# Joint seven-product pairs over both sequences for the mixing projections of an encoder layer

## The chip, the cores and the metric

One core of a Trainium2 chip runs the whole layer. The metric is device microseconds of one execution, and the median of three executions is given. A profile comes from one more execution, traced by the hardware profiler.

## What is computed

The layer works on two sequences of 512 tokens with 1024 channels, each by itself but with the same weights, in float32. Cut to what matters here:

```python
x = x + 0.5 * swiglu(rms_norm(x, ffn1_norm), ...)          # D_FF = 2816
h = rms_norm(x, mix_norm)
aq, ak, av, mq, mk, mv, gate_pre, o_pre, g_att, g_mlstm = split(h @ w_in)
#   widths 512 128 128 512 512 512 16 512 1024 1024
att = gqa_block_attention(rope(rms(aq)), rope(rms(ak)), av)  # 8 heads of 64, 2 key heads
mem = mlstm_bidirectional(mq, mk, mv, gate_pre, gate_bias, o_pre, head_norm)   # 4 heads of 128
merged = sigmoid(g_att) * (att @ w_up_att) + sigmoid(g_mlstm) * (mem @ w_up_mlstm)
x = x + merged @ w_out
x = x + 0.5 * swiglu(rms_norm(x, ffn2_norm), ...)
```

mlstm_bidirectional ends with a norm per head, a per-channel weight (head_norm) and sigmoid(o_pre) as a gate.

## The kernel before

**Matrix products.** A float32 operand is split in two parts, hi and lo, and a product is the sum of three TensorE matmuls (hi·hi, hi·lo, lo·hi) of 128x128 by 128x512. Activations lie transposed, channels on partitions, so a column block of 128 output channels over one sequence is 8 x 3 = 24 matmuls. The split is one ACT copy and one DVE subtraction. Split weights that are wanted again are parked in DRAM by load_w (L247) and fetched back by the second sequence.

**The order.** First loads and transposes, then the first FFN up (class Up, `product` at L333), FFN down (L589), then mix(0) and mix(1), which are generators for the two sequences, interleaved by hand at the end of the kernel, then the second FFN. Both FFNs take the two sequences together and use the seven products of Strassen and Winograd in place of eight half-size products: the sequences are one axis of the 2x2 split, the halves of the 1024 input channels the second, and two column blocks the third. Their operands are the split tiles `xc[B11]`, `xc[B21]`, `xc[B22]`, `xc[T1]` to `xc[T4]`, split from normalised rows by `put` (L278 on ACT, L279 on DVE). Each product is 12 matmuls. An Up object keeps the results of some blocks that it began early in DRAM.

**mix.** The first sequence's rows come out of FFN down one column block at a time. There they are only scaled by the norm's channel weight and split into `xh`, `xl` (emit_hl, L143); the factor per token (`r[s]`, and `R[s]` for the transposed layout) is applied where a projection leaves PSUM. The squares for the norm are taken by ACT (L152) and added by POOL (L156). Then follow, per sequence:

- kv and gates (272 columns) and q (512 columns) by tok_proj, tokens on partitions (L739);
- rope on q and k (L787 to L808, L928), transposes to `qT` and `kst`;
- attention, eight heads: scores (L989 to L1004: matmuls at L995, the maximum over a row of 512 at L998, exponentials at L1000, the reciprocal at L1001 and the scaling at L1002), then attend (L1006 to L1032: transposes at L1014, split of what they give at L657 by ACT and L658 by DVE, matmuls at L1021);
- mLSTM, four heads: mask rows out of DRAM (L961), mem_head (L1098; exponentials at L1122, products with the scores at L1124), mem_out (L1141, matmuls at L1157, square at L1159, normalisation to L1164);
- merges (merge_att, merge_mem), the projection `w_up` of attention and memory, gated;
- the output projection in eight units (out_unit, L1188).

The 28 column blocks of `w_in` (8 of the attention gate, 8 of the memory gate, 4 of the output gate, 8 of the mLSTM's q and k) go through proj and proj_w (L755). They are units, of which each has a load and a computation. `go` runs units with the load one unit ahead, and `queue` with `fill(n)` puts n units between other work. This is how the blocks lie between the heads of attention and mLSTM:

```python
queue.extend(att_gate(d) for d in range(KD))
queue.extend(out_gate(h) for h in range(2))
Ps = scores(0)
for h in range(HA):
    nxt = scores(h + 1) if h + 1 < HA else None
    attend(h, Ps)
    Ps = nxt
    mem_max(h // 2, h % 2)
    fill(1 if h < 4 else 2)
```

Engines take their instructions in the order of a scheduler's priorities; `shifted(n)` moves what is under it by n places. All DMAs are issued by SP.

## Time and profile before

| | |
|---|---|
| median of three executions | 2101.9 us (2101.75 to 2104.15) |
| profiled execution | 2103.76 us, span 2101.90 us |
| mean granted TensorE clock | 0.996 |
| PE busy | 2067.3 us, 98% of the span, 9488 matmuls and transposes |
| DVE, ACT, POOL busy | 1577.5, 895.6, 104.6 us |

Of a group the profile gives the line, engine, operation, output and input tiles, shapes and count, then busy time and the mean of one, and behind the second bar the idle time of the engine in front of the group and what ended it. A line of the timeline has the start and the length in us, then the same names; a bracket holds the idle time before it and its releaser. A row of windows has the stretch, its length, the busy time (and number of instructions) of PE, PEld, DVE, ACT and POOL, then the granted clock, the share of DMA and GB/s.

By the timeline, FFN down ends at 658 us and the second FFN's products begin at 1448.75. Between these lie, as far as they can be parted: kv and q of the first sequence 658 to 693, its rope and attention to 828, its mLSTM and merges to 1011, kv and q of the second to 1044, the output projection of the first and rope of the second to 1113, attention of the second to 1222, its mLSTM to 1346, memory gate and merge to 1405, and its output projection.

### The profile page before, as it was taken

To read this page: it belongs to the slowest core of one execution; us is meant where nothing else is said; L and a number is where in the kernel's file an instruction comes from. 1 tells how busy PE (TensorE), PEld (TensorE's weight loads), DVE (VectorE), ACT (ScalarE), POOL (GpSimd) and SP (SyncE) were. 2 spreads that over 40 slices of the span, in tenths; PEclk is the share of its full clock that TensorE was granted. 3 is DMA by queue.
4 is the path that set the end of the run, shared out by engine and by line. 5 is a ranking of instruction groups with operands and counts; after the bars stand their busy time and mean duration, and the time that the engine had idled before them with its cause. 6 is when DMAs were issued, how large, how long until landed. Compare 5 with 4: busy or idle time off the path is not lost.

```text
span 2101.9 us, 27326 instructions
## 1 busy us (share of the span) xinstructions
PE 2067.3 (98%) x9488; PEld 1693.5 (81%) x9488; DVE 1577.5 (75%) x2864; ACT 895.6 (43%) x1643; POOL 104.6 (5%) x112
## 2 busy tenths in 40 slices
PE   8999999999999999999999999999999999999997
PEld 6888888888888777878887787788888888888886
DVE  7888888786797898575568745554888888786796
ACT  6544444442234566463344543323544444442222
POOL 0000000001003011000110000001000000000000
PEclk9999999999999999999999999999999999999999
DMA  8655655699767654778585354677656555599752
GB/s 275 203 172 191 194 176 177 210 353 343 262 228 253 203 186 161 252 255 277 186 291 178 103 171 144 216 243 239 206 170 224 179 183 181 179 353 341 268 191 110
DMA packets 304186, 458.53 MB, mean 218 GB/s; under 512 B 20304, under 2 KB 170848, under 8 KB 303024
## 3 DMA queue, kind: packets, MB, share of 16 engines
q1 hardware_dynamic: 303456, 455.52, 64.4%
q0 software_dynamic: 592, 1.27, 0.3%
q8 instruction: 75, 1.23, 0.2%
q14 instruction: 63, 0.52, 0.1%
HBM read 289.82 MB, written 166.89 MB: 217 GB/s over the span
## 4 chain that ended last, share of the span: by engine, by line
PE 91%; DVE 5%; DMA 2%; ACT 1%; issue 1%; SPq 0%; POOL 0%; DVEq 0%; ACTq 0%; POOLq 0%
PE pss L333 17%; PE mm L755 17%; PE pst L333 11%; PE mm L333 11%; PE mm L589 8%; PE pst L589 4%; PE pss L589 4%; PE mm L739 4%; PE pso L589 3%; PE pso L1021 1%; PE pso L739 1%; PE pst L1014 1%; PE pso L1157 1%; PE pss L995 1%; PE pst L755 1%; PE pss L755 1%
## 5 line engine op out<-in xcount | busy, mean ns | idle before, releaser
L755 PE MATMUL mm<-xh,w 128*128 128x512 f32 x896 | 291.5, 395 | 0.5 <-DMA w<-wpark 0.5
L333 PE MATMUL pss<-xc,w 128*128 128x512 f32 x1056 | 256.2, 391 | 0.7 <-DVE t L364 0.7
L333 PE MATMUL mm<-xc,w 128*128 128x512 f32 x1056 | 253.0, 390 | 2.5 <-DVE xc L279 1.0
L333 PE MATMUL pst<-xc,w 128*128 128x512 f32 x1056 | 253.6, 389 | 0.0
L333 PEld LDWEIGHTS pss<-xc,w 128*128 128x128 f32 x1056 | 196.9, 188 | 47.9 <-DVE t L364 7.3
L333 PEld LDWEIGHTS mm<-xc,w 128*128 128x128 f32 x1056 | 197.4, 188 | 45.4 <-DVE w L292 1.5
L333 PEld LDWEIGHTS pst<-xc,w 128*128 128x128 f32 x1056 | 198.2, 188 | 41.2
L755 PEld LDWEIGHTS mm<-xh,w 128*128 128x128 f32 x896 | 167.8, 189 | 34.0 <-DMA w<-wpark 1.2
L589 PE MATMUL mm<-rt,w 128*128 128x512 f32 (+1 forms) x819 | 187.7, 383 | 0.0
L755 PE MATMUL mm<-xl,w 128*128 128x512 f32 x448 | 176.3, 394 | 0.0
L589 PEld LDWEIGHTS mm<-rt,w 128*128 128x128 f32 x819 | 150.6, 188 | 29.8
L291 ACT ACTIVATE w<-t 128x512 fp32r<-128x512 f32 x176 | 107.0, 627 | 139.1 <-issue 55.2
L292 DVE TENSOR_TENSOR w<-t,w 128x512 fp32r<-128x512 f32 x176 | 118.2, 687 | 54.9 <-ACT w L291 53.0
L333 PE MATMUL pss<-xc,f 128*128 128x512 f32 x528 | 126.8, 389 | 0.0
L333 PEld LDWEIGHTS pss<-xc,f 128*128 128x128 f32 x528 | 99.1, 188 | 20.6
L657 ACT ACTIVATE w<-wr 128x512 fp32r<-128x512 f32 x72 | 45.2, 632 | 137.7 <-PE pso L589 71.8
L755 PEld LDWEIGHTS mm<-xl,w 128*128 128x128 f32 x448 | 84.4, 188 | 16.2
L657 ACT ACTIVATE w<-t 128x512 fp32r<-128x512 f32 x82 | 51.8, 632 | 107.3 <-PE pst L589 62.4
L589 PE MATMUL pst<-rt,w 128*128 128x512 f32 x396 | 93.7, 389 | 0.0
L589 PE MATMUL pss<-rt,w 128*128 128x512 f32 x396 | 93.7, 389 | 0.0
L239 ACT ACTIVATE w<-wr 128x1024 fp32r<-128x1024 f32 (+1 forms) x56 | 57.2, 1028 | 71.8 <-PE mm L755 34.0
L589 PEld LDWEIGHTS pss<-rt,w 128*128 128x128 f32 x396 | 74.3, 188 | 15.4
(331 smaller groups left out, 3686.9 us busy)
## 6 DMA issues: line engine op xcount, KB each, us to landing
rt<-rbuf SPq DMA_DIRECT2D x154, 512.0 KB, 5.3
wpark<-w SPq DMA_DIRECT2D x104, 512.0 KB, 3.2
w<-wpark SPq DMA_DIRECT2D x104, 512.0 KB, 4.9
wr<-in_ffn_w_gate_dram SPq DMA_DIRECT2D x62, 512.0 KB, 5.5
rbuf<-tab SPq DMA_DIRECT2D x102, 256.0 KB, 4.1
wr<-in_ffn_w_up_dram SPq DMA_DIRECT2D x44, 512.0 KB, 4.6
rbuf<-f SPq DMA_DIRECT2D x72, 256.0 KB, 4.0
wr<-in_w_in_dram SPq DMA_DIRECT2D x36, 512.0 KB, 6.5
```

What stands on the lines that cost most here:

```text
L239: pin(nc.scalar.activation(hi, raw, AF.Copy))
L291: pin(nc.scalar.activation(t[:, 0], src, AF.Copy))
L292: pin(V_.tensor_tensor(t[:, 1], src, f(t[:, 0]), op=ALU.subtract))
L333: nc.tensor.matmul(p, a[:, k, :], xt[:, b, k, :], start=(first and k == 0 and i == 0), stop=(k == HK_ - 1 and i == 2), skip_group_check=True)
L589: nc.tensor.matmul(p, u[:, a, d * P:(d + 1) * P], r[:, b, ts], start=(first and q == 0 and k == 0), stop=(q == len(us) - 1 and k == 2), sk ...
L657: nc.scalar.activation(hi, src, AF.Copy)
L739: nc.tensor.matmul(p[b][:, :N], a[:, k, bs], w_[:, kl, :], start=(k == 0 and i == 0), stop=(k == KD - 1 and i == 2))
L755: nc.tensor.matmul(p, a[:, k, :], b, start=(k == 0 and i == 0), stop=(k == n - 1 and i == 2))
L995: nc.tensor.matmul(p, qT[:, h, b * P:(b + 1) * P], kv[:, hk * 2 + j, :], start=(j == 0), stop=(j == 1))
L1014: nc.tensor.transpose(p[:, b * P:(b + 1) * P], Ps[b][:, kb * P:(kb + 1) * P], ident)
L1021: nc.tensor.matmul(po, Vst[:, kv_, hk, :], w, start=(kv_ == 0 and i == 0), stop=(kv_ == 3 and i == 1))
L1157: nc.tensor.matmul(po, vm[:, a, t, hs_], b, start=(t == 0 and n == 0), stop=(t == 3 and n == 2))
```

## The change

The 28 column blocks leave mix. A new class Joint, derived from Up, computes them in a stage of its own between the first FFN and mix, as 14 pairs of blocks over both sequences, seven products to a pair; nine pairs are begun early on `xc[B11]` and `xc[B21]` alone. Gate blocks leave it as tanh of half their value, q and k blocks split in hi and lo, all into DRAM (`agbuf`, `mgbuf`, `ogbuf`, `qkbuf`). Attention and mLSTM fetch them from there.

For this the rows are normalised in place before the stage, so the factor per token goes from all later evictions. done1 takes the first sequence's norm at the end of FFN down and writes `xc[B11]`, `xc[B21]`; the second sequence's statistics follow behind the first pair's first products. The lower half of the second sequence's rows, which the stage uses only in sums, is saved split in DRAM (`xlbuf`) and fetched afterwards. kv and q of both sequences are then computed together, q and k of the second resting unrotated in `rawbuf`; mLSTM's values of the second sequence come next (they fill rope of the first, and rest in `vbuf`), and those of the first are the filler of its attention, in two halves (tok_halves). Output units of the first sequence are the filler in rope (four) and attention (three) of the second. The `1 +` of the output gate and head_norm move from POOL into two DVE instructions of mem_out. An added one-element exponential in `gates` is to have ACT's table loaded before attention. The rest of the second FFN is the same.

```diff
+    QK_, TANH_ = 0, 1
+    JOINT = 9
+    class Joint(Up):
...
+            n = len(blocks)
+            begun, whole = list(range(JOINT - LAST)), list(range(JOINT, n))
+            self.order = [j for p in zip(begun, whole) for j in p]
+            self.order += begun[len(whole):] + whole[len(begun):] + list(range(JOINT - LAST, JOINT))
...
+        def out(self, j, i, s, src, row=None):
+            _, kind, to = self.blocks[j][i]
+            lo = src if row is None else row
+            if kind == TANH_:
+                nc.scalar.activation(lo, src, AF.Tanh, scale=0.5)
+                nc.sync.dma_start(to(s), lo)
+                return
+            hi = self.ring("o")
+            nc.scalar.activation(hi.bitcast(F32R), src, AF.Copy)
+            V_.tensor_tensor(lo.bitcast(F32R), src, hi, op=ALU.subtract)
+            nc.sync.dma_start(to(s)[:, 0, :], hi)
+            nc.sync.dma_start(to(s)[:, 1, :], lo)
...
+        def begin(self, j, W):
+            self.kept[j] = kept[j][0]
+            t = self.ring("o")
+            X = gu_first_a(W, self.xc, t)
+            nc.sync.dma_start(kept[j][0], t)
+            self.begun()
+            self.open = j, X, W
+        def begun(self):
+            if self.open:
+                j, X, W = self.open
+                product(X, W[B21], self.xc[B21], False)
+                self.out(j, 0, 0, X, self.ring("o"))
+            self.open = None
...
+            Y, Z = PS(), PT()
+            second = lambda: product(Y, W[T2_], xc[T2_], True)
+            v1 = got or ring("v")
+            if got:
+                second()
+            else:
+                X = gu_first_a(W, xc, v1)
+                second()
+                product(X, W[B21], xc[B21], False)
+                with shifted(SOONER):
+                    self.out(j, 0, 0, X, ring("h"))
+            u2, v5 = ring("h"), ring("v")
+            with shifted(SOONER):
+                V_.tensor_tensor(u2, v1, Y, op=ALU.add)
+            product(Z, W[T1], xc[T1], True)
+            with shifted(SOONER):
+                nc.scalar.activation(v5, Z, AF.Copy)
+            mid()
+            product(Y, W[T3], xc[T3], False)
+            with shifted(SOONER):
+                V_.tensor_tensor(v5, v5, Y, op=ALU.add)
+            with shifted(SOONER):
+                V_.tensor_tensor(v5, v5, v1, op=ALU.add)
+            self.out(j, 1, 1, v5)
+            product(Z, W[B22], xc[B22], False)
+            with shifted(SOONER):
+                V_.tensor_tensor(u2, u2, Z, op=ALU.add)
+            self.out(j, 0, 1, u2)
+            product(Y, W[T4], xc[T4], False)
+            with shifted(SOONER):
+                V_.tensor_tensor(v1, v1, Y, op=ALU.add)
+            self.out(j, 1, 0, v1)
...
+    KK = 2
+    KORDER = (4, 6, 0, 2)
+    def tok_load(cols, k0):
+        return load_w([win_v[:, k0:k0 + KK, c:c + n] for c, n in cols], ("in", cols[0], k0))
+    def tok_part(p, x, w, k0, blocks, N):
+        for kl in range(KK):
+            xh, xl = x(k0 + kl)
+            for b in blocks:
+                bs = slice(b * P, (b + 1) * P)
+                for i, (a, w_) in enumerate(((xh, w[0]), (xh, w[1]), (xl, w[0]))):
+                    nc.tensor.matmul(p[b][:, :N], a[:, bs], w_[:, kl, :],
+                                     start=(k0 == KORDER[0] and kl == 0 and i == 0),
+                                     stop=(k0 == KORDER[-1] and kl == KK - 1 and i == 2))
...
+            for x, p in zip(xs_, ps_):
+                tok_part(p, x, w, k0, range(4), N)
+            if k0 == KORDER[-1]:
+                for done, p in zip(dones, ps_):
+                    for b in range(4):
+                        done(b, p[b])
...
+    def tok_halves(x, cols, done):
...
+        def comp(half, k0):
+            blocks = (2 * half, 2 * half + 1)
+            if k0 == KORDER[0]:
+                p.update((b, MM()) for b in blocks)
+            tok_part(p, x, ws[k0], k0, blocks, N)
+            if k0 == KORDER[-1]:
+                for b in blocks:
+                    done(b, p[b])
+        return [((lambda h=h, k0=k0: load(h, k0)), (lambda _, h=h, k0=k0: comp(h, k0)))
+                for h in range(2) for k0 in KORDER]
...
-    OUT = 3
-
-    def mix(s, xh, xl, early=None, extra=None, after=None):
-
-        xsrc = lambda k: (xh[:, k, :], xl[:, k, :])
+    def mix(s, rope_fill, att_fill, extra=None, after=None):
...
+        def v_done(b, p):
+            hi, lo = [F2(F32R) for _ in range(2)] if s else (vm[:, 0, b, :], vm[:, 1, b, :])
+            split(p, hi, lo)
+            if s:
+                for i, t in enumerate((hi, lo)):
+                    nc.sync.dma_start(vbuf[:, i, b, :], f(t))
+        qks, ogs = {}, {}
+        def mem_fetch(h):
+            qks[h] = wpool.tile([P, 4, S], F32R, tag="w8", bufs=4, name=nm("qk"))
+            nc.sync.dma_start(f(qks[h]), qkbuf[s][h])
+            ogs[h] = T2(F32, "ac")
+            nc.sync.dma_start(ogs[h], ogbuf[s][:, h, :])
...
-        go(*tok_proj(xh, xl, [(512, 256), (2304, 16)], 2, kv_done))
-        if early:
-            early()
-        go(*tok_proj(xh, xl, [(0, 512)], 2, q_done), mem_qk(0, 0))
-        yield None
+        yield kv_done, k_rope, q_done, v_done
+        if s:
+            k_rope()
         gates()
-        k_turn()
+        if not s:
+            k_turn()
         for b in range(4):
+            if s:
+                qraw.append(raw_row(b))
             q_rope(b)
-        yield None
-        go(mem_qk(0, 1), mem_qk(1, 0), mem_qk(1, 1))
...
+        queue.extend(att_fill)
+        fill(1)
         Ps = scores(0)
         for h in range(HA):
             nxt = scores(h + 1) if h + 1 < HA else None
             attend(h, Ps)
             Ps = nxt
             mem_max(h // 2, h % 2)
-            fill(1 if h < 4 else 2)
-            if h == 2 and extra:
+            fill(1)
+            if h == 3 and extra:
                 extra()
         mem_scales()
         fill(99)
+        for d in range(KD):
+            nc.sync.dma_start(mg[:, d, :], agbuf[s][:, d, :])
+        for h in range(2):
+            mem_fetch(h)
...
+        def gate_fetch(d):
+            t = ths[d] = T2()
+            nc.sync.dma_start(t, mgbuf[s][:, d, :])
...
-            V_.tensor_tensor(og, og, po, op=ALU.mult)
+            V_.scalar_tensor_tensor(og, og, 1.0, po, op0=ALU.add, op1=ALU.mult)
             rh = rstd_cols(col_sums(h2), 4, DM)
-            Rh = bcast_psum(rh)
-            V_.tensor_tensor(og, og, Rh, op=ALU.mult)
-            split(og, mem[:, h, 0, :], mem[:, h, 1, :])
+            with shifted(160):
+                Rh = bcast_psum(rh)
+                V_.scalar_tensor_tensor(og, og, hn[:, h:h + 1], Rh, op0=ALU.mult, op1=ALU.mult)
+                split(og, mem[:, h, 0, :], mem[:, h, 1, :])
...
         for h in range(HM):
             Ts = mem_head(h)
-            if h == 0:
-                go(*mem_values())
             queue.append(merge_att(2 * h))
             fill(1)
             mem_out(h, Ts)
             if h + 2 < HM:
-                queue.extend([out_gate(h + 2), mem_qk(h + 2, 0), mem_qk(h + 2, 1)])
+                mem_fetch(h + 2)
             queue.append(merge_att(2 * h + 1))
             fill(99)
 
         mh, ml = A([P, KD, S], F32R, "mh"), A([P, KD, S], F32R, "ml")
-        go(*[mem_gate(d) for d in range(KD)])
         go(*[merge_mem(d) for d in range(KD)])
-        flush()
-        yield None
...
     def done1(s, d, _):
-        if s == 0:
-            if d == 0:
-                nhl[0] = xhl_tiles()
-            emit_hl(xs[0][:, d, :], gm, d, *nhl[0])
         nc.sync.dma_start(xbuf[s][:, d, :], xs[s][:, d, :])
         accs[s] = sq_add(xs[s][:, d, :], accs[s], "R")
         if s == 0 and d == KD - 1:
-            mid_stats(0, 100, 140)
-
-    def mid_stats(s, a=0, b=0):
-        with shifted(a):
-            r[s] = stats(accs[s])
-        with shifted(b):
-            R[s] = bcast_cols(r[s])
-
-    r = [None, None]
-    R = [None, None]
-
-    def prep1(d):
-        if d == 0:
-            nhl[1] = xhl_tiles()
-        xt = T2(F32, "f2")
-        nc.sync.dma_start(xt, xbuf[1][:, d, :])
-        emit_hl(xt, gm, d, *nhl[1])
+            with shifted(100):
+                r = stats(accs[0])
+            with shifted(140):
+                R = bcast_cols(r)
+                xc[B11], xc[B21] = xc_tile(), xc_tile()
+                for k in range(KD):
+                    normed(xs[0][:, k, :], gm, R, k)
+                    put(xc[B11 if k < HK_ else B21], k % HK_, xs[0][:, k, :])
...
-    m0 = mix(0, *nhl[0], None, lambda: mid_stats(1), prep1)
-    for _ in range(3):
-        next(m0)
...
+    def qk_block(h, i):
+        return (768, 1280)[i] + h * P, QK_, lambda s: qkbuf[s][h][:, 2 * i:2 * i + 2, :]
+    def tanh_block(c, buf, d):
+        return c + d * P, TANH_, lambda s: buf[s][:, d, :]
+    blocks = [[tanh_block(2832, agbuf, d + i) for i in range(2)] for d in range(0, KD, 2)]
+    blocks += [[tanh_block(3856, mgbuf, d + i) for i in range(2)] for d in range(0, KD, 2)]
+    blocks += [[tanh_block(2320, ogbuf, d + i) for i in range(2)] for d in range(0, HM, 2)]
+    blocks += [[qk_block(h, i) for i in range(2)] for h in range(HM)]
+    up = Joint(xc, blocks)
+    W = [up.left(0)]
+    up.begin(0, W[0])
+    r1 = stats(accs[1])
+    W += [up.left(j) for j in (1, 2)]
+    R1 = bcast_cols(r1)
+    up.begin(1, W[1])
+    up.begin(2, W[2])
+    for i in (B22, T1, T2_, T3, T4):
...
+    for k in range(HK_):
+        x0l, x0u, x1l, x1u = [xs[s][:, k + i * HK_, :] for s in range(2) for i in range(2)]
+        normed(x1l, gm, R1, k)
+        normed(x1u, gm, R1, k + HK_)
+        for j in ((3,), (4, 5), (6,), (7, 8))[k]:
+            up.begin(j, up.left(j))
+        put(xc[B22], k, x1u)
+        t3, t4 = up.ring("x"), up.ring("x")
+        V_.tensor_tensor(x0l, x1l, x0l, op=ALU.subtract)
+        V_.tensor_tensor(t3, x1u, x1l, op=ALU.subtract)
+        V_.tensor_tensor(x1u, x1u, x0l, op=ALU.subtract)
+        V_.tensor_tensor(t4, x0u, x1u, op=ALU.subtract)
+        put(xc[T1], k, x0l)
+        put(xc[T2_], k, x1u)
+        hi, lo = up.ring("s"), up.ring("s")
+        split(x1l, hi.bitcast(F32R), lo.bitcast(F32R))
+        nc.sync.dma_start(xlbuf[:, 0, k, :], hi)
+        nc.sync.dma_start(xlbuf[:, 1, k, :], lo)
+        later.append((T3, k, t3))
+        later.append((T4, k, t4))
...
+    up.rest(raw0)
...
-    m1 = mix(1, *nhl[1], None, lambda: stats2(0), prep2)
-    next(m1)
-    next(m0)
-    next(m1)
-    acc2[0] = next(m0)
-    next(m1)
-    next(m1)
-    acc2[1] = next(m1)
+    def extra():
+        acc2[0] = outs0[1][0]
+        stats2(0)
+    box()
+    ms = [mix(s, fills[0][s], fills[1][s], (None, extra)[s], (None, prep2)[s]) for s in range(2)]
+    (kv0, kr0, q0, v0), (kv1, kr1, q1, v1) = [next(m) for m in ms]
+    go(*tok_proj(src, [(512, 256), (2304, 16)], (kv0, kv1)))
+    go(*tok_proj(src, [(0, 512)], (q0, q1)))
+    first, *units = tok_proj(src[1:], [(1792, 512)], (v1,))
+    go(first)
+    kr0()
+    fills[0][0][:3] = [[u] for u in units]
+    fills[1][0].extend(tok_halves(src[0], [(1792, 512)], v0))
+    outs0 = next(ms[0])
+    go(*outs0[0][:1])
+    fills[0][1][:] = [[u] for u in outs0[0][1:5]]
+    fills[1][1].extend(outs0[0][5:])
+    box()
+    outs1 = next(ms[1])
+    go(*outs1[0])
+    flush()
+    acc2[1] = outs1[1][0]
```

217 lines of the change are left out of this document (118 added, 99 removed).

## The prediction

> **What bounds the kernel now.** I read the page first, then the chain of waits, then busy time by windows over the mixing part.
>
> ```profile
> L755 PE MATMUL mm<-xh,w 128*128 128x512 f32 x896 | 291.5, 395 | 0.5 <-DMA w<-wpark 0.5
> ...
> L755 PE MATMUL mm<-xl,w 128*128 128x512 f32 x448 | 176.3, 394 | 0.0
> ```
>
> These are the matmuls of the 28 column blocks, one of the page's largest groups, with next to no idle time in front. The 395 ns is the latency of one matmul, not its price. The price comes from the chain of waits, where a long unbroken stretch stands:
>
> ```profile
> 1405.39 43.52 PE mm L755 x192
> ```
>
> 43.52/192 is 226.7 ns per 128x512 matmul. So a removed matmul is worth 0.2267 us where PE alone sets the pace. The windows tell where it does:
>
> ```profile
> 658.00:693.00 35.00, 34.85 (x199) 30.44 (x197) 20.34 (x44) 18.62 (x34) 12.65 (x17) 1.00 0.97 329
> 693.00:828.00 135.00, 129.60 (x651) 102.36 (x649) 125.26 (x258) 80.12 (x159) 14.68 (x11) 1.00 0.54 175
> ...
> 1113.00:1222.00 109.00, 104.32 (x508) 83.04 (x506) 82.90 (x188) 55.07 (x119) 0.70 (x1) 0.98 0.42 136
> ```
>
> The columns are PE, PEld, DVE, ACT, POOL, clock, DMA. 658 to 693 is kv and q of the first sequence: PE alone, as in the output projection of the second, the 43.52 us above. 693 to 828 is rope and attention of the first sequence, with ten column blocks as filler between the heads: DVE is busy 125.26 of 135 us, so here DVE sets the pace and PE is full only because filler lies in the gaps. In the second attention (1113 to 1222) DVE has 82.90 of 109: PE sets it. The part that changes lies between these rows of the timeline:
>
> ```profile
> 658.03 0.41 PE L739 MATMUL mm<-w,xh 128*128 128x272 f32 x2
> ...
> 1448.75 2.88 PE L333 MATMUL mm<-xc,w 128*128 128x512 f32 x12
> 1452.45 0.66 PE L203 MATMUL pst<-ident,R 128*128 128x128 f32 x4 [0.82 <-POOL R L156]
> 1452.86 0.94 PE L333 MATMUL mm<-xc,w 128*128 128x512 f32 x3
> ```
>
> From 658.0 (first kv matmul) to 1448.7 (second FFN) are 790.7 us. Four transposes cost 0.41 (1452.45 to 1452.86). I take the rest of the program as unchanged and build the same stretch anew.
>
> **What is removed.** The 28 blocks are 28 x 2 x 24 = 1344 matmuls, the two L755 rows above (896+448). Seven products for a pair over both sequences are 7 x 12 = 84, 14 pairs 1176. That is 168 fewer, 168 x 0.2267 = 38.1 us. This is the whole gain, and it holds only if PE is as full afterwards. It cannot be: the blocks were the filler of attention and of the mLSTM heads, and they move to a stage of their own (266.6 us). I therefore go through the stages.
>
> **Seam after the first FFN.** Before, the first sequence's projection starts on unnormalised x, with the scale applied afterwards, and the second's statistics are wanted much later. Now the new stage needs normalised x at once. ACT and POOL at that place before:
>
> ```profile
> 657.55 1.34 ACT L239 ACTIVATE w<-wr 128x544 fp32r<-128x544 f32 x2 [4.51 <-PE pso L589]
> 658.79 0.62 ACT L152 ACTIVATE R<-xs 128x512 f32<-128x512 f32 x1
> ...
> 659.54 11.75 POOL L156 TENSOR_TENSOR R<-R,f 128x512 f32<-128x512 f32 x7 [12.75 <-ACT R L152]
> ```
>
> ACT stood behind a weight split that waits for the last FFN matmuls to free a weight buffer; only then came the first square of the second sequence, and POOL needed 11.75 us for seven additions (1.68 each), to 671.3. The changed program's order has the same two weight splits (now 128x1024, two of them) ahead of that square, then squares that wait for POOL to free their buffers, and between these the first copy into xc, and on PE the transposes of the second sum right behind 13 matmuls of the new stage. By these rows: first square at 660, additions end at 672; the first xc copy stands behind two squares that wait for two additions, 664. PE idles 658 to 664.4, does 13 matmuls, idles again until 672. That is 14 us with 3 us of work, 11 lost, and 1 more where the T1 weights are ready late. **12 us.** Bounds: 2 if the squares are not held up, 16 if the whole of the chain from 656 to 672 lies bare.
>
> A gap of that length has a second price:
>
> ```profile
> 1120.12 0.85 PE L995 MATMUL pss<-kv,qT 128*128 128x512 f32 x2 [4.47 <-ACT t L1000]
> ...
> 1120.60:1123.90 3.30, 3.30 (x11) 2.49 (x10) 3.30 (x9) 1.70 (x6) 0.00 (x0) 0.50 1.02 388
> ```
>
> After 4.47 us idle (the gap in brackets) the granted clock was 0.50 over the 3.3 us from 1120.60 on, a loss of about 1.7. At the seam the first such stretch would run into the wait for POOL and cost nothing, the second may or may not come; the 12 stands, with 1.7 more in the bound. [...]
>
> **New stage.** 1176 x 0.2267 = **266.6**. A pair costs 19.0 us (84), a pair begun earlier 13.6 (60). By the program's order DVE has 9 splits and sums of 512 elements, 5 additions, at most one split of 1024 and, for q/k pairs, 4 more splits. DVE prices, from one start to the next in the timeline:
>
> ```profile
> 765.71 1.27 DVE L998 TENSOR_REDUCE asm<-pss 128x1 f32<-128x512 f32 x2
> 766.91 1.27 DVE L658 TENSOR_TENSOR t<-pst,t 128x512 fp32r<-128x512 f32 x2
> ...
> 770.62 0.21 DVE L1001 RECIPROCAL asm<-asm 128x1 f32<-128x1 f32 x2
> 770.75 0.15 DVE L171 TENSOR_SCALAR rs<-rs 128x4 int32<-128x4 int32 x1
> 770.81 0.48 DVE L1002 TENSOR_SCALAR t<-t,asm 128x512 f32<-128x512 f32 x1
> 771.21 0.16 DVE L173 TENSOR_SCALAR rs<-rs 128x4 int32<-128x4 int32 x1
> ```
>
> Two maxima of 512 elements took 1.20 (765.71 to 766.91), so 0.60 each, and the two splits behind them, at 1.27 with the last one's tail, no more; the scaling took 0.40 (770.81 to 771.21), a reciprocal about 0.07. Thus at most 18 x 0.60, and 1.2 for the split of 1024, 12 us against 13.6 to 19.0: hidden. The results' DMAs, 1 to 2 MB a pair, are hidden by the same 19 us.
>
> **kv and q of both sequences.** Two of the 35 us windows: **70**.
>
> **Attention of the first sequence.** Filler now: the value projection of both sequences, 96 matmuls each; by the program's order the first fills rope, of the second half lies in heads 0 to 2, the other half behind the last scores, because the value tile waits for q's buffer. Heads 3 to 7 have none. A head's DVE work: 4 maxima, 4 splits, 1 addition, 2 gate maxima, half a split, 11.5 x 0.60, 4 x 0.40, 4 x 0.08 = 8.8 us, against PE's 16 matmuls (3.6) and 16 transposes (1.6). The scaling was slower in this stage:
>
> ```profile
> L1002 DVE TENSOR_SCALAR t<-t,asm 128x512 f32<-128x512 f32 x32 | 19.7, 619 | 0.1
> ...
> L657 ACT ACTIVATE t<-pst 128x512 fp32r<-128x512 f32 x32 | 18.9, 595 | 13.3 <-PE pst L1014 12.3 <-DVE asm L998 1.0
> L240 DVE TENSOR_TENSOR w<-wr,w 128x1024 fp32r<-128x1024 f32 x13 | 16.1, 1235 | 0.8 <-ACT w L239 0.8
> ```
>
> 619 against 480 ns adds 0.6 a head. Behind the last scaling DVE waits for transposes (0.41) and ACT's copy (0.60), with no other work queued: 0.9. Period 10.3, eight heads 82; entry 28 (21.8 of value matmuls, 12 groups of transposes, 5), exit 5: **115**. The other way: 135 before, less 13 weight splits (16.1), 17 gate and q/k passes (10.2), plus 8 value splits (4.8) and 4 weight splits (5.0) gives 118.5. Bounds 103 (8.8 a head) and 122.
>
> **mLSTM of the first sequence.** Three blocks a head, two heads, and the value projection are gone as filler; what is left is 24 merge matmuls a head. What a head takes with little filler, from 1308 on:
>
> ```profile
> 1309.58 0.29 DVE L1124 SCALAR_TENSOR_TENSOR t<-pss,t 128x128 f32<-128x128 f32 x1
> ...
> 1324.63 0.28 DVE L1124 SCALAR_TENSOR_TENSOR t<-pss,t 128x128 f32<-128x128 f32 x1
> ...
> 1345.76 0.69 DVE L1164 TENSOR_TENSOR box<-box,pst 128x512 f32<-128x512 f32 x1 [0.20 <-PE pst L213]
> ```
>
> ```profile
> 1323.82 5.96 ACT L1122 ACTIVATE t<-box,st 128x128 f32<-128x128 f32 x20
> ...
> 1340.51 0.60 ACT L1159 ACTIVATE t<-pso 128x512 f32<-128x512 f32 x1 [1.34 <-PE pso L1157]
> ```
>
> 15.05 us lie between two heads' first products on DVE, and 17.3 from the start of a head's 20 exponentials to the end of its square on ACT (1341.1), behind which a next head's exponentials would stand, as they do in the changed order. Some work of other kinds lay in between, so I take 16.2, and 7 from the last square to the end of the last split, two DVE passes behind 1345.76. 4 x 16.2 + 7 = 71.8; 69 of the 96 merge matmuls stand behind that on PE's queue, 15.7: **87.5** (82 to 93).
>
> **The rest.** Five output blocks (27.2) and 12 groups of transposes (4.9) cover rope of the second sequence: **33**, with 1 of loss. Attention of the second: 9.4 of DVE a head (the mask addition is on DVE here), 0.9 of wait, 82, exit 4: **86** (75 to 109). mLSTM as above plus the mask rows:
>
> ```profile
> L961 DVE TENSOR_TENSOR box<-box,tab 128x512 f32<-128x512 f32 x6 | 4.1, 689 | 10.0 <-DMA box<-ebuf 10.0
> ```
>
> DVE stood 10.0 us for them in the second mLSTM before; there it was covered by blocks. Now splits queue behind: **89** (83 to 98). Output projection **43.5**.
>
> **Sum.** 12 + 266.6 + 70 + 115 + 87.5 + 33 + 86 + 89 + 43.5 = 802.6, against 790.7: 12 us slower. The profiled execution took 2103.8 with a span of 2101.9; the median of the three runs is 2101.9, 1.9 below the profiled one's time, and I add the difference to the median: **2114 us**. The 38.1 us are earned and some 50 are paid in DVE-paced attention, bare mLSTM chains and the seam.
>
> **Rivals.** *DVE stays fed* (not slower). In attention DVE's wait of 0.9 and the slow scaling vanish, since PE and ACT, freed of filler, answer at once: 8.8 and 9.4 a head, 12 + 7 less; with mLSTM heads at 15.05, 9 less. 2095 to 2086. For it: DVE was 93% busy at 693 to 828 even with filler in PE's queue. Against: DVE's queue is in order and its next entry after the last scaling is the split that waits. It decides at a head period under about 9.5 us.
> *Fetches come late.* q/k tiles, gate rows and mask rows come from DRAM in front of bare chains; at the 10.0 us of the L961 row for each sequence: 2134. For it: SP's one queue. Against: they are issued a head ahead.
> *The clock falls in attention.* If a bare head leaves PE a gap like the 4.47 us one, each head loses 1.7: 16 heads, 27, 2141. Against: the gaps that I expect are 1 to 2 us. [...]
> *The new stage does not hold its rate*, its outputs waiting for buffers: 1 us a pair, 2128.
>
> **Chances.** Forecast 0.52, its own range 2102 to 2126, with a tenth of it on either side; DVE stays fed 0.25; fetches late 0.13; new stage 0.06; clock 0.04. About 0.2% (4.2 us) is what a measurement here can tell from no change. A fifth of the forecast's case, 0.10, lies in that band and 0.03 below it: faster 0.28, same 0.10, slower 0.62. The range takes in the fed case and the fetches: 2086 to 2134.
>
> **What would show it.** Right: 1176 matmuls in the new stage at 0.2267 us; a PE gap of 5 us or more at the seam, ended by ACT's xc copy, then by POOL; heads 3 to 7 of the first attention at 10 us with PE half empty; mLSTM heads near 16. Wrong: heads at 9 us or less, no seam gap, or PE above 97% between the new stage and the second FFN.

## The result and the profile after

The changed kernel is slower: 2186.4 us, median of three (2183.8 to 2189.1), against 2101.9; the ratio is 1.0397 with a 95% interval of 1.0382 to 1.0413. The forecast of 2114 (2086 to 2134) had the sign and a seventh of the size. The profiled execution, the slowest of the three, took 2189.09 us with a span of 2187.3, that is 85.4 more span than before.

From the page of the changed kernel, the busy times of all engines, and the clock in 40 slices:

```profile
span 2187.3 us, 27410 instructions
## 1 busy us (share of the span) xinstructions
PE 2078.6 (95%) x9320; PEld 1686.2 (77%) x9320; DVE 1680.7 (77%) x3038; ACT 942.8 (43%) x1745; POOL 102.9 (5%) x104
...
PEclk9999999999998999999999997989999999999999
```

PE has 168 instructions less than before and is busy 11.3 us longer (2067.3 before). At the pace of 0.2267 the missing matmuls are 38.1 us, so what is left takes 49.4 us longer. Part of that is half clock: over the span the granted clock is 0.972, against 0.996 before. Part may be that matmuls which stand apart count with their whole length (0.39 us for a single one, 0.2267 in an unbroken row); no run parts the two. The time in which PE does nothing grew from 34.6 (2101.9 less 2067.3) to 108.7. Thus -38.1 + 49.4 + 74.1 = 85.4, the whole difference.

Busy time by windows, one row for each term of the prediction's sum (length, then PE, PEld, DVE, ACT, POOL, clock, DMA share, GB/s):

```profile
658.00:938.50 280.50, 272.43 (x1185) 223.47 (x1186) 201.57 (x305) 121.88 (x202) 11.15 (x7) 0.98 0.55 169
938.50:1006.00 67.50, 67.50 (x386) 60.00 (x385) 17.00 (x35) 25.40 (x55) 3.69 (x20) 1.00 0.60 205
1006.00:1128.20 122.20, 107.59 (x520) 81.88 (x519) 109.73 (x255) 66.37 (x147) 13.39 (x10) 0.94 0.40 128
1128.20:1232.90 104.70, 88.00 (x384) 66.02 (x383) 84.73 (x220) 59.40 (x137) 18.87 (x11) 0.92 0.62 213
1232.90:1282.30 49.40, 44.53 (x227) 36.02 (x226) 38.09 (x81) 19.31 (x34) 7.42 (x5) 1.00 0.89 296
1282.30:1384.40 102.10, 76.78 (x325) 52.06 (x323) 82.66 (x189) 51.40 (x116) 4.09 (x4) 0.85 0.42 131
1384.40:1490.30 105.90, 88.47 (x364) 67.22 (x363) 75.34 (x226) 50.92 (x130) 0.00 (x0) 0.85 0.53 169
1490.30:1533.60 43.30, 43.30 (x193) 35.86 (x192) 16.63 (x23) 11.06 (x16) 9.08 (x6) 1.00 0.75 264
```

| stage | forecast | measured |
|---|---|---|
| seam and new stage | 278.6 | 280.5 |
| kv and q, both sequences | 70 | 67.5 |
| attention of the first | 115 | 122.2 |
| mLSTM of the first | 87.5 | 104.7 |
| output of the first, rope of the second | 33 | 49.4 |
| attention of the second | 86 | 102.1 |
| mLSTM of the second | 89 | 105.9 |
| output projection | 43.5 | 43.3 |
| sum | 802.6 | 875.6 |

The new stage, kv, q and the output projection came as forecast; all 73 us of the miss lie in the five stages between, from which the filler was taken. There the granted clock is 0.85 to 1.00 and PE has 5 to 25 us without work in each.

Inside these stages the misses lie unevenly. This is the first attention cut where the value products of its first head end, then the second cut where those of its fifth head end:

```profile
1006.00:1061.90 55.90, 52.37 (x270) 42.04 (x269) 53.09 (x129) 26.20 (x57) 9.51 (x7) 1.00 0.65 212
1061.90:1128.20 66.30, 55.22 (x252) 39.84 (x251) 56.64 (x127) 40.17 (x90) 3.88 (x3) 0.90 0.18 56
...
1282.30:1364.00 81.70, 60.19 (x241) 40.51 (x239) 65.70 (x155) 37.25 (x85) 4.09 (x4) 0.81 0.50 158
1364.00:1384.40 20.40, 16.59 (x84) 11.55 (x84) 16.96 (x35) 14.16 (x32) 0.00 (x0) 1.00 0.09 23
```

In the first attention the value products of the next six heads end 8.8 to 11.7 us apart, 10.5 in the mean, as priced (10.3), and the last comes 4.0 behind. The miss is in front of them: rope and the first head take 55.9 where 28 and 10.3 were counted, with DVE busy for 53.1. In the second attention the last three heads come at 8.8, 8.1 and 3.9, below the price, and the five before them, beside the first of which the last output units and their rows lie, take 81.7 where five heads at 10.3 are 51.5.

**The seam.** The timeline of PE behind the first FFN:

```profile
662.60 1.22 PE L333 MATMUL mm<-xc,w 128*128 128x512 f32 x2 [6.04 <-ACT xc L278]
665.32 1.65 PE L333 MATMUL mm<-xc,w 128*128 128x512 f32 x3 [1.50 <-DVE xc L279]
668.68 4.19 PE L333 MATMUL mm<-xc,w 128*128 128x512 f32 x8 [1.71 <-DVE xc L279]
```

A gap of 6.04 us ended by ACT's first copy into xc, then two more ended by DVE's part of that split, where a wait for POOL was forecast. POOL added from 658.13 to 669.75, and in that time each of these DVE operations took about 1.7 us (0.68 behind it). 280.5 less 266.6 for 1176 matmuls leaves 13.9; 12 was forecast, with the half clock in the bound. So the size was right, and the path only in its first half.

**Attention of the second sequence.** PE, DVE, ACT and SP from its timeline:

```profile
1299.92 0.60 PE L1155 MATMUL pst<-ident,t 128*128 128x128 f32 x4
1307.91 2.08 PE L1136 MATMUL pss<-kv,qT 128*128 128x512 f32 x4 [7.39 <-ACT t L1141]
...
1305.70 0.69 DVE L1327 SCALAR_TENSOR_TENSOR f<-mm,f 128x512 f32<-128x512 f32 x1 [3.08 <-DMA f<-xbuf]
...
1306.42 0.63 ACT L155 ACTIVATE t<-f 128x512 f32<-128x512 f32 x1 [5.71 <-DVE f L1327]
1307.08 0.69 ACT L1141 ACTIVATE t<-pss,asm 128x512 f32<-128x512 f32 x1
...
1295.93 3.17 SPq L1192 DMA_DIRECT2D mg<-agbuf  x7
1299.20 0.38 SPq L1326 DMA_DIRECT2D f<-xbuf  x1
```

Read from below: SP issued seven fetches of gate rows and then the residual row of an output unit. DVE's residual sum (L1327) waited for it, ACT's square of that sum (L155) stood in front of the next head's exponentials (L1141), and PE's next scores waited for those: 7.39 us. An output unit that was meant as cover carried a wait into the chain.

**mLSTM of the first sequence.** PE, DVE and POOL between two heads:

```profile
1174.97 0.84 PE L899 MATMUL mm<-att,w 128*128 128x512 f32 x3
1178.96 0.93 PE L213 MATMUL pst<-ident,rs 128*128 128x128 f32 x4 [3.15 <-DVE rs L192]
1179.89 1.60 PE L1287 MATMUL pst<-ident,t 128*128 128x128 f32 x4
...
1174.17 1.23 DVE L240 TENSOR_TENSOR w<-wr,w 128x1024 fp32r<-128x1024 f32 x1
1175.31 1.24 DVE L190 TENSOR_TENSOR rs<-rs,rs 128x4 f32<-128x4 f32 x1
...
1176.55 1.21 DVE L240 TENSOR_TENSOR w<-wr,w 128x1024 fp32r<-128x1024 f32 x1
1177.69 1.21 DVE L192 SCALAR_TENSOR_TENSOR rs<-rs,rs 128x4 f32<-128x4 f32 x1
...
1174.93 3.95 POOL L1103 TENSOR_TENSOR box<-box,tab 128x512 f32<-128x512 f32 x2 [16.54 <-DMA box<-ebuf]
```

In PE's queue the transposes that spread the last head's norm (L213) stand ahead of the next head's (L1287). They wait for small DVE steps, between which lie two weight splits, and two of these steps of four elements take 1.2 us each. Before, 24-matmul blocks lay in this place.

### The profile page after: what moved, and what is told of

The parts are those of the page before. It is cut to its first block, busy times and chain, and to the rows that moved or that the text cites. A ratio compares the mean times of both kernels' runs of the same rounds, so it can differ in the third digit from the quotient of the medians.

```text
span 2187.3 us, 27410 instructions
## 1 busy us (share of the span) xinstructions
PE 2078.6 (95%) x9320; PEld 1686.2 (77%) x9320; DVE 1680.7 (77%) x3038; ACT 942.8 (43%) x1745; POOL 102.9 (5%) x104
## 4 chain that ended last, share of the span: by engine, by line
PE 82%; DVE 10%; DMA 4%; ACT 3%; issue 1%; SPq 0%; POOL 0%; DVEq 0%; ACTq 0%; POOLq 0%
PE pss L333 22%; PE pst L333 14%; PE mm L333 12%; PE mm L700 8%; PE pst L700 4%; PE pss L700 4%; PE mm L899 4%; PE pso L700 3%; PE mm L846 2%; DMA box<-ebuf 1%; PE pso L1295 1%; DVE t L769 1%; ACT t L1260 1%; PE pst L1155 1%; DVE asm L1139 1%
## 5 line engine op out<-in xcount | busy, mean ns | idle before, releaser
L333 PE MATMUL mm<-xc,w 128*128 128x512 f32 x1392 | 335.4, 393 | 11.7 <-ACT xc L278 6.8
L333 PE MATMUL pss<-xc,w 128*128 128x512 f32 x1392 | 337.2, 391 | 0.5 <-DVE t L364 0.3
L333 PE MATMUL pst<-xc,w 128*128 128x512 f32 x1392 | 334.7, 389 | 0.0
L333 PEld LDWEIGHTS mm<-xc,w 128*128 128x128 f32 x1392 | 261.7, 189 | 69.9 <-ACT xc L278 7.7
L333 PEld LDWEIGHTS pss<-xc,w 128*128 128x128 f32 x1392 | 259.9, 188 | 61.1 <-DVE t L364 6.9
L333 PEld LDWEIGHTS pst<-xc,w 128*128 128x128 f32 x1392 | 261.3, 188 | 54.2
L291 ACT ACTIVATE w<-t 128x512 fp32r<-128x512 f32 x232 | 140.8, 627 | 158.7 <-issue 55.2
L292 DVE TENSOR_TENSOR w<-wr,w 128x1024 fp32r<-128x1024 f32 x58 | 70.9, 1223 | 31.9 <-ACT w L291 31.9
L700 PEld LDWEIGHTS pst<-rt,w 128*128 128x128 f32 x396 | 74.3, 188 | 15.4
L769 DVE TENSOR_TENSOR t<-pst,t 128x512 fp32r<-128x512 f32 x96 | 64.9, 686 | 26.5 <-ACT t L768 25.6
L291 ACT ACTIVATE w<-wr 128x1024 fp32r<-128x1024 f32 x58 | 61.1, 1056 | 50.3 <-PE pst L333 21.6
```

The costliest lines, as they stand in the source:

```text
L291: pin(nc.scalar.activation(t[:, 0], src, AF.Copy))
L292: pin(V_.tensor_tensor(t[:, 1], src, f(t[:, 0]), op=ALU.subtract))
L333: nc.tensor.matmul(p, a[:, k, :], xt[:, b, k, :], start=(first and k == 0 and i == 0), stop=(k == HK_ - 1 and i == 2), skip_group_check=True)
L700: nc.tensor.matmul(p, u[:, a, d * P:(d + 1) * P], r[:, b, ts], start=(first and q == 0 and k == 0), stop=(q == len(us) - 1 and k == 2), sk ...
L769: (eng or V_).tensor_tensor(lo, src, f(hi), op=ALU.subtract)
```

## The experiments

Each group of runs has its own runs of the kernel before beside it, so I compare ratios: the last column is the difference to the changed kernel's 1.0397, times 2102 us. (Where an expectation names 8.3 and 9.4 for e1 and e3, it took differences of medians.)

| run | median us | ratio, 95% interval | against the changed kernel, us |
|---|---|---|---|
| e1_fill24 | 2178.1 | 1.0351 (1.0334 to 1.0369) | -9.7 |
| e2_thin_before | 1991.4 | 0.9466 (0.9452 to 0.9480) | (before, changed) |
| e3_rows_early | 2177.0 | 1.0351 (1.0336 to 1.0367) | -9.7 |
| e4_norm_later | 2187.4 | 1.0400 (1.0384 to 1.0415) | +0.6 |
| e5_cover_all | 2164.3 | 1.0291 (1.0275 to 1.0307) | -22.3 |
| e6_gates_back | 2177.4 | 1.0358 (1.0343 to 1.0373) | -8.2 |
| e7_thin_first | 2094.3 | 0.9963 (0.9951 to 0.9976) | (before, changed) |
| e8_splits_ahead | 2179.8 | 1.0385 (1.0359 to 1.0411) | -2.5 |
| e9_mask_dve | 2178.0 | 1.0373 (1.0352 to 1.0394) | -5.0 |
| e10_raw_ahead | 2179.7 | 1.0379 (1.0363 to 1.0396) | -3.8 |
| e11_four_mends | 2162.6 | 1.0297 (1.0280 to 1.0314) | -21.0 |
| e12_mends_gates | 2154.7 | 1.0251 (1.0234 to 1.0268) | -30.7 |

My theory after the result: matmuls taken from a stretch that DVE and ACT pace are not worth their pace there, and PE's idle time then costs a second time, since it halves the granted clock (0.50 in 16 stretches of the mixing part). The rivals: waits alone, or the time is still PE's.

**Work added.**

```diff
             queue.append(merge_att(2 * h))
             fill(1)
+            spare(vm[:, 0, 0, 0:P], vm[:, 0, 1, :], 24)
             mem_out(h, Ts)
```

> The changed kernel with 24 more matmuls (128x512, on tiles that are there anyway, results unused) in each of the eight mLSTM heads: 192, which at 0.2267 us are 43.5 us more of TensorE work. Theory 'waits and clock' (the heads are bare, TensorE idles in them, and the idle time halves the granted clock for what follows): the added work lies in the idle time and brings the clock back; 0 to 20 us faster than the changed kernel, the clock at 1.00 through the mLSTM heads. Theory 'waits alone' (the half clock falls on time in which TensorE waits anyway): 0 to 10 us slower. Theory 'TensorE sets the pace of these heads': 43 us slower.

43.5 us more work made the kernel 9.7 us faster. The two mLSTM stretches by windows:

```profile
1130.90:1233.00 102.10, 99.93 (x477) 79.18 (x476) 83.00 (x221) 60.27 (x137) 17.63 (x11) 1.00 0.64 215
1386.80:1484.00 97.20, 87.71 (x413) 68.23 (x413) 76.50 (x226) 51.21 (x129) 0.00 (x0) 0.98 0.56 184
```

The clock is 1.00 and 0.98 where it was 0.92 and 0.85, and 96 added matmuls fit into each. PE does not set the pace of these heads, and the theory of waits alone expected 0 to 10 us slower: this speaks for a half clock that costs time. A rival is left: the scheduler also put other instructions in another order (on DVE, ACT and PE, in both stretches), and no run parts that from the clock.

**Work taken from the kernel before.**

```diff
         def win_cols(c0, done):
-            return proj(win_v[:, :, c0:c0 + P], ("in", c0), xsrc, KD, done)
+            return proj(win_v[:, :, c0:c0 + P], ("in", c0), xsrc, 1, done)
```

> The kernel before, with every column block cut to the first of its eight channel tiles: 3 matmuls instead of 24, so 56 x 21 = 1176 matmuls less, which is 266.6 us at 0.2267; weights, splits and evictions stay. It leaves out seven eighths of these sums. By the prediction's pricing (bare heads at 10.3 and 16.2 us) the stretch would fall by about 230 us. Theory 'waits and clock' (bare heads cost what they cost in the changed kernel: its stretch without the new stage and the seam is 595 us against 791): about 195 us or less, with the granted clock falling in attention and mLSTM. If TensorE alone set the pace: 266 us.

1176 matmuls less, 266.6 us at their pace, saved 111.4 us (2102.84 to 1991.41): 0.095 us each, two fifths of the pace, far less than any of the figures expected. But 0.095 is a mean of very different stretches. The first attention, from first scores to last value products, before and thinned:

```profile
717.50:830.00 112.50, 108.86 (x535) 85.38 (x534) 103.96 (x214) 69.82 (x143) 11.71 (x9) 1.00 0.54 176
```

```profile
713.20:835.40 122.20, 92.12 (x358) 63.72 (x357) 107.12 (x223) 71.76 (x147) 13.57 (x10) 0.78 0.52 168
```

With 177 PE instructions less this stretch became 9.7 us longer, at a clock of 0.78. Behind the second mLSTM, where the eight blocks of its memory gate run beside merges and the output projection, before and thinned:

```profile
1340.50:1449.00 108.50, 108.24 (x482) 89.27 (x482) 41.07 (x71) 23.27 (x37) 9.09 (x6) 1.00 0.67 221
```

```profile
1262.00:1337.80 75.80, 71.48 (x314) 57.51 (x314) 39.41 (x71) 23.12 (x37) 9.08 (x6) 1.00 0.86 303
```

Here 168 matmuls less saved 32.7 us, 0.195 each, close to the pace. This is the price list that the prediction should have had: next to nothing for a block between the heads of the first attention, nearly the pace for one in a stretch of its own. What the thinned kernel keeps (splits and evictions of the blocks, on DVE and ACT) the changed kernel does not have, so it got back more than 111.4: 195.6 us (790.7 before, 875.6 less 280.5 after); it paid 280.5.

**The first attention alone.** The same cut for the ten blocks there only:

```diff
-            return win_cols(2832 + d * P, done)
+            return win_cols(2832 + d * P, done, 1 if s == 0 else KD)
...
-            return win_cols(2320 + h * P, done)
+            return win_cols(2320 + h * P, done, 1 if s == 0 and h < 2 else KD)
```

> The kernel before with the ten column blocks that fill the first sequence's attention cut to 3 of 24 matmuls, all else as it was: 210 matmuls less, 47.6 us of TensorE work. It leaves out seven eighths of these sums. Theory 'clock' (in the kernel thinned everywhere this stretch, from the first scores to the last value products, went from 112.6 to 122.1 us, with 68 us of it at half clock): 4 to 12 us slower than before. Theory 'waits alone': unchanged to 10 us faster, since DVE was busy 125 of 135 us there. TensorE's price: 48 us faster.

It was 7.7 us faster, not slower. The stretch itself:

```profile
715.90:829.20 113.30, 86.75 (x358) 60.64 (x357) 104.53 (x216) 70.29 (x143) 13.07 (x10) 0.86 0.58 189
```

113.3 against 112.5: 177 of the 210 matmuls, 40.1 us at the pace, are gone from it (358 PE instructions against 535), nothing is gained, and a clock of 0.86 cost nothing visible either. The gain of 7.7 came behind it, in the mLSTM, before and now:

```profile
830.00:951.50 121.50, 120.72 (x568) 96.70 (x567) 84.88 (x211) 68.17 (x145) 11.48 (x9) 1.00 0.76 249
```

```profile
829.20:943.20 114.00, 113.23 (x534) 90.46 (x534) 83.46 (x210) 67.11 (x145) 10.60 (x8) 1.00 0.76 252
```

The other matmuls lay there: 34 PE instructions less saved 7.5 us, their full pace (7.7), since PE is busy all the time. So in this attention DVE (104.5 us busy) sets the time and the half clock falls on waits: "waits alone" is right here, and my clock theory was too broad. Why the fully thinned kernel is 9 us longer in the same stretch with nearly the same work isn't settled.

**Late fetches.**

```diff
+            def first():                     # with the unit's weights, one unit ahead
+                rows.append(T2(F32, "f2"))
+                nc.sync.dma_start(rows[0], xbuf[s][:, d, :])
+                return load()
-                xt = T2(F32, "f2")           # in done, behind the matmuls
-                nc.sync.dma_start(xt, xbuf[s][:, d, :])
```

> The changed kernel, with the residual rows of an output unit fetched with the unit's weights, one unit ahead, instead of when its matmuls are done. Theory 'late rows' (in the second attention DVE's in-order queue stands at the sum that waits for its row, behind it the exponentials and the scores: a gap of 7.39 us on TensorE, others of 1.3 to 3.0, and 31 us at half clock): 8 to 18 us faster than the changed kernel, the gap of 7.39 gone. Theory 'the chain of a bare head sets it': under 3 us.

9.7 us faster; the gap of 7.39 is gone, and the second attention took 94.8 instead of 102.1, its clock 0.89 instead of 0.85:

```profile
1282.90:1377.70 94.80, 74.24 (x323) 51.77 (x321) 81.06 (x188) 51.67 (x117) 3.83 (x3) 0.89 0.45 138
```

The other suspected queue, SP behind the rows of the second FFN:

```diff
-    ms = [mix(s, fills[0][s], fills[1][s], (None, extra)[s], (None, prep2)[s]) for s in range(2)]
+    ms = [mix(s, fills[0][s], fills[1][s], (None, extra)[s]) for s in range(2)]
...
-    go(*outs1[0])
+    for d in range(KD):
+        prep2(d)
+        go(outs1[0][d])
```

> The changed kernel, with the normalised rows of the first sequence for the second FFN (fetch, scale, store, split) made beside the last output units instead of in the merges and heads of the second mLSTM. Theory 'SP queue' (two groups of these DMAs held SP for 11.7 and 10.7 us, and the merge weights behind them came late: gaps of 2.54 and 3.29 us on TensorE that end on DMA): 5 to 14 us faster. Theory 'the head's own chain sets it': no change within 3 us. If the second FFN then waits for its rows: slower by up to 8.

No change in the median (+0.6). The two gaps of PE that end on the merge weights' DMA are still there, 5.7 us in all where the changed kernel has 5.8, so the rows of the second FFN were not what made these weights late; what did is open.

**Cover everywhere.** e3 and e1 together, and in the second attention:

```diff
             fill(1)
+            if s and 1 < h < 7:
+                spare(kv[:, 0, 0:P], kv[:, 1, :], 16)
```

> The changed kernel with three things at once: the residual rows early, the 24 spare matmuls in each mLSTM head, and 16 spare matmuls in each of five heads of the second attention; 272 spare matmuls, at 0.2267 us 61.7 us of TensorE work whose results are unused. Theory 'waits and clock': the two gains seen so far, 8.3 and 9.4, add up, and the five heads bring a little more: 2160 to 2172 us, the clock at half in the second attention nearly gone. Theory 'TensorE has become the bound once it is covered': 2178 or more.

2164.3, as expected. The second attention, from its first scores to its last value products, went from 94.8 with the rows early to 89.3, at full clock:

```profile
1278.50:1367.80 89.30, 88.28 (x446) 69.19 (x444) 81.38 (x190) 51.16 (x117) 3.86 (x3) 1.00 0.48 154
```

Against e3 this kernel does 61.7 us more work and is 12.6 us faster (1.0351 less 1.0291). If the clock is the cause (the order of instructions changed here too), it costs the changed kernel at least that. At most it costs 42, by an estimate: these are the 16 stretches of the changed kernel's mixing part at a clock of 0.50, and what PE was busy in them, which full clock could have halved:

```profile
sum 105.84, PE 84.05 PEld 60.00 DVE 72.87 ACT 39.50 POOL 11.55; mean PE 5.25 PEld 3.75 DVE 4.55 ACT 2.47 POOL 0.72
```

So the clock is the smaller part of the 85. At almost full clock (0.989 over the span) e5 is still 61 us behind the kernel before.

**Part of the change undone.**

```diff
-    blocks = [[tanh_block(2832, agbuf, d + i) for i in range(2)] for d in range(0, KD, 2)]
...
+    go(*[gate_unit(1, d) for d in range(KD)])                 # second sequence, behind q
...
+    fills[1][0].extend(gates0 + halves)                       # first: filler in attention, fill(2)
```

> The changed kernel with the four pairs of the attention gate taken out of the new stage: the first sequence's eight gate blocks are filler in its attention heads again (24 matmuls each, on the tiles that stand there), the second sequence's eight are computed behind q. Against the changed kernel that is 336 matmuls less in the new stage, 192 plain and 192 as filler more: 48 more in all, 10.9 us by the pace. Theory 'cover' (a block in a bare stretch costs what the thinned kernel before showed, 111 us for 1176 matmuls, or 0.095 us each): -76.2 + 43.5 + 18 = 15 us faster than the changed kernel, and heads of the first attention without half clock. Theory 'TensorE's work counts': 11 us slower.

8.2 us faster with 48 matmuls more. "TensorE's work counts" is out; of the 15 us that "cover" expected, half came. From its first scores to its last value products the first attention took 116.5 us instead of 91.4: 25.1 for 192 matmuls, 0.131 each where 0.095 was counted, beside an attention that has the value projection too.

**Three smaller mends, alone and together.** Merge weights split beside kv and q; mask additions on DVE; the raw rows fetched at once.

```diff
+    for n, u in enumerate(tok_proj(src, [(512, 256), (2304, 16)], (kv0, kv1))):
+        go(u, parks[n])          # parks: load_w of ("up", part, d), no computation; so for q
```

```diff
-            (G_, V_)[s].tensor_tensor(em3, ...
+            V_.tensor_tensor(em3, ...
```

```diff
             k_rope()
+            qraw.extend(raw_row(b) for b in range(4))
...
-            if s:
-                qraw.append(raw_row(b))
             q_rope(b)
```

> The changed kernel with the merge weights split and put into DRAM beside kv and q (where DVE is busy 17 of 68 us), so that the first mLSTM fetches them split; its DVE loses eight splits of 1024, two a head, which stood between the small steps of the head's norm. Theory 'splits on the chain': heads of the first mLSTM go from 20 to the 17 to 18 us that the second sequence's show: 6 to 10 us faster. Theory 'the chain of exponentials, products and transposes sets the head': under 3 us. If the added 12 MB crowd the weights of kv and q: slower by up to 8.

> The changed kernel with the first sequence's mask additions on DVE (0.60 us each) instead of POOL. Theory 'DVE waits for POOL' (two 4-element steps of the norm took 1.25 and 1.21 us in a head, and ended as POOL's addition ended; 0.16 elsewhere): 2.2 us less and 1.2 us more DVE a head, and in attention 0.6 more a head: 0 to 5 us faster. Theory 'these steps are off the chain': 0 to 8 us slower, DVE having 16 additions more.

> The changed kernel with the second sequence's raw q rows fetched all at once ahead of its rope, not each when the row before is done. Theory 'late raw rows' (DVE stood 3.24, 1.38 and 0.33 us for them, TensorE 1.69 and 0.92 us behind that): 3 to 7 us faster, attention of the second sequence starting that much earlier. Theory 'the output units fill that stretch, and attention then lacks them': under 3 us.

> The changed kernel with the residual rows early, the merge weights split ahead, the mask additions on DVE and the raw rows ahead, all at once, no spare work. If the gains add: 9.4 + 8 + 2 + 4, about 2163. If they overlap, since each only lays bare the next wait of a bare head: 2168 to 2176.

Alone they gave 2.5, 5.0 and 3.8 us, each within or at the edge of its interval. With e3's 9.7 the sum is 21.0, and the four together gave 21.0 (2162.6). As far as intervals of 3 to 5 us tell, they add and do not merely uncover each other; how the 11.3 beside e3's divide among the three is not shown. In e8 the heads of the first mLSTM did come at 16 to 18 us (the last products of its heads end at 1148.2, 1165.8, 1182.9 and 1198.6), where the changed kernel has 18 to 22 (1146.2, 1166.7, 1188.6, 1206.7).

The four mends and e6 in one kernel:

> The four mends and the attention gate's blocks back as cover (first sequence's as filler, second's behind q), so ten pairs in the new stage instead of fourteen. If cover still pays once the late fetches are gone: 9 us less than the four mends alone, about 2153. If the filler now meets a DVE that is busy without a pause in the first attention: 2158 to 2166. Before stays ahead in either case by 50 us or more, since the new stage pays in full for matmuls that cost two fifths of that as filler.

2154.7 us, as the first case has it: 9.7 us less than the four mends (1.0297 less 1.0251) and still 2.5% behind the kernel before. No version of the new stage that was tried beats it.

## Why the prediction was wrong, step by step

- **Bound and stages.** That PE paces the projections and DVE the first attention, so that moved blocks lose their cover, was right, and so was the sign. The new stage at 0.2267 us a matmul, the seam with its first gap ended by ACT (the second by DVE, not by POOL), kv, q and the last projection were right within 3 us each; from 668.7 to 938.5 PE had no gap over 0.3. Of the signs named, heads 3 to 7 of the first attention at 10 us came, PE half empty did not (busy 55.2 of 66.3 us behind the first head), and mLSTM heads near 16 did not.
- **The failed step is the pricing of the five stages that lost their filler**: 410.5 forecast, 484.3 measured. The price of a bare head of attention, 10.3, held or was high (10.5 in the first; 8.8 and 8.1 at the end of the second). What failed is the entry of the first attention (28, measured 45.6 if the first head is taken at 10.3), the first five heads of the second (51.5, measured 81.7), the heads of mLSTM (16.2, measured 17 to 22) and rope of the second (33, measured 49.4). I summed each stage from DVE's instructions and one wait and took the engines to answer at once. The sum of DVE's busy time was about right (82.7 of 102.1 in the second attention, against my 9.4 a head, 75), but the time between its instructions was not: it waits in turn for rows, for PE at half clock and for ACT. A head here goes through three engines in turn, and the largest busy time did not give its time: the first five heads of the second attention took 81.7 us, with DVE busy for 65.7, PE for 60.2 and ACT for 37.3.
- **What the runs put a number to.** The four mends together are worth 21.0 us, covering with spare work 12.6 beside e3; the two were not run together. Some 40 of the 73.8 are left that no run assigns to a cause.
- **Attention of the first**, 115 forecast and 122.2 measured, lay at its bound of 122 (the second way of counting gave 118.5). Its entry was counted by PE's work, value matmuls and transposes, which add up to 26.8 and not 28. By the rows DVE paces it: busy 53.1 of the first 55.9 us with rope and the first head, it waited 2.3 for a mask row and never for PE, while PE's gaps there, 3.5 in all, end on DVE. Rope's work on DVE was in no term of that sum, and PE had more to do than counted as well (busy 52.4). That the heads behind came below their term (66.3 against 77) hid most of this, which is luck. Both mLSTM stretches passed their upper bounds (93 and 98), the second attention stayed within its 109.
- **mLSTM heads.** 16.2 was taken from a stretch of before in which, with the filler there, the clock was still 1.00 (1308 to 1346). With spare work and the clock back, e1's second sequence shows 16.7 to 17.6 between the ends of heads' products, its first still 17.6 to 20.1; with the first sequence's splits ahead, e8 shows 15.7 to 17.6. So clock and splits are parts of the 18 to 22; their shares, and POOL's, were not measured apart.
- **Rope, 33.** Not a wait in the main: PE was busy 44.5 of 49.4. More output units than five ran there (158 of their matmuls, 6.6 units; their loads were a unit ahead, and, as I take it, nothing else was ready), and the second attention lacked them.
- **The rivals.** "Fetches come late" (0.13, 10 us a sequence) did come true, on rows that I had not named: residual rows (9.7), perhaps raw rows (3.8, at the edge of its interval). Of those that I named, DVE stood 10.1 us for mask rows over both sequences, ACT 1.7 for a gate row, and no engine's wait ends on a q/k tile. It was no alternative to the forecast but an addition to it. "The clock falls in attention" (0.04) came true too, mostly on much shorter gaps than I required, though in the first attention of e7 it cost nothing visible. I put rivals side by side that have one cause, bare heads, and so come together; adding 20 and 27 to 2114 would have given 2161, still 25 short.
- **Short gaps.** Against the clock's fall I had only set that the gaps I expected, 1 to 2 us, are shorter than the 4.47 us of the kernel before. That such gaps leave the clock alone was my estimate, and the trace does not bear it out: 14 of the 16 falls in the mixing part come at gaps of 0.8 to 3.3 us, the other two at 6.04 and 7.39 (below).

Open: how the remaining 53 us of e12 divide within the heads, whether a smaller seam or another place for the stage would change the sign, and the 9 us between the two thinned kernels in the first attention. A stage for fewer pairs, with the second sequence's blocks as filler too, wasn't tried. By an estimate from e2, the memory gate's pairs alone would about break even: 96 matmuls at 0.195 are 18.7 us, and a pair costs 19.0 in the new stage, the seam's 13.9 not counted.

## What to carry to other kernels

Here the pace of a matmul, 0.2267 us, was its price only where PE was the bound (0.195 behind the second mLSTM, nothing in the first attention); before moving filler out of a stretch that another engine paces, cut it to a few instructions in the kernel as it is and measure what that saves. Look at it stretch by stretch: 40.1 us of matmuls were worth nothing in the first attention and 7.7 were worth 7.5 in the mLSTM behind it. Here 266.6 us of matmuls were worth 111.4, and 195.6 with their splits and evictions gone too, so a new stage that pays 280.5 for them loses. Filler that carries its own fetch into a queue that is worked off in order isn't only cover: fetching its row ahead gave 9.7 us.

## What the hardware showed that I had not expected

**The clock fell behind short gaps.** Windows of the changed kernel, two pairs from the first attention and one from rope of the second sequence (columns as above; the clock stands behind POOL):

```profile
1073.38:1076.79 3.41, 1.35 (x6) 0.71 (x5) 3.35 (x8) 2.67 (x7) 0.00 (x0) 1.00 0.00 0
1076.79:1083.62 6.83, 6.25 (x22) 4.77 (x22) 5.19 (x18) 2.85 (x7) 0.00 (x0) 0.50 0.01 2
...
1104.10:1107.51 3.41, 1.95 (x8) 0.78 (x5) 3.29 (x10) 3.13 (x7) 0.00 (x0) 1.00 0.02 5
1107.51:1110.92 3.41, 2.75 (x11) 2.46 (x12) 2.34 (x5) 0.60 (x1) 0.00 (x0) 0.50 0.00 0
...
1237.22:1240.63 3.41, 1.45 (x11) 1.20 (x12) 3.41 (x9) 0.63 (x1) 0.00 (x0) 1.00 0.67 238
1240.63:1244.04 3.41, 3.41 (x17) 2.79 (x16) 3.41 (x13) 0.74 (x1) 0.00 (x0) 1.00 0.56 190
```

The clock went to 0.50 behind a window of 3.41 us in which PE had been busy 1.35 us, its longest gap there 1.31 (in front of the scores at 1076.18), and behind one of 1.95. In the third pair 1.45 busy did not do it, so busy time alone doesn't tell. The stretches at half clock in the mixing part last 3.41 to 13.65 us, in steps of 3.41. Cut the whole mixing part at these edges, and of the windows at full clock all ten with PE busy for 1.35 us or less have half clock behind them, six of eleven with 1.45 to 1.95, and none with 2.03 or more (PE's ends are modelled, so the bounds are rough).

**Small DVE steps took 1.2 us while POOL added.** In the mLSTM rows above two DVE steps on four elements, L190 and L192, took 1.24 and 1.21 us inside POOL's additions, and the same two 1.25 and 1.21 in the head before; all other steps of these two lines on four elements in the mixing part took 0.12 to 0.16. In e9, with the additions moved to DVE, no such step took longer than 0.17, and the kernel was 5.0 us faster, which its interval does not part from zero.
